# The convolution's banded matrices read from memory one by one, instead of being multiplied out on VectorE

## The chip, the cores and the metric

The kernel runs on one core of a Trainium2 chip. The metric is the device time of one execution in microseconds (us), lower is better. Three executions of the kernel before gave 2970.77, 2972.89 and 2979.89 us; the median is 2972.89 us. TensorE (PE in the profile) multiplies matrices, VectorE (DVE) and ScalarE (ACT) do the elementwise work, GpSimd (POOL) and SyncE (SP) mostly issue transfers. Each engine takes its own instructions in a fixed order.

## The reference, cut to what matters

Two layers over 1024 latent tokens and 256 context tokens, width 1024. The first layer's token mixer is a Conformer convolution module; the second is attention; each is followed by a SwiGLU feed-forward block. The change touches the depthwise convolution of the first layer alone:

```python
CONV_WIDTH = 31; CONV_PAD = 15
def conv_module(h, w_pw1, b_pw1, w_dw, b_dw, ln_g, ln_b, w_pw2, b_pw2):
    u = h @ w_pw1 + b_pw1                       # 1024 -> 2048
    a, gt = jnp.split(u, 2, axis=-1)
    u = a * jax.nn.sigmoid(gt)
    u = lax.conv_general_dilated(               # every channel has 31 taps of its own
        u, w_dw[:, None, :], window_strides=(1,), padding=[(15, 15)],
        dimension_numbers=("NWC", "WIO", "NWC"), feature_group_count=u.shape[-1]) + b_dw
    u = jax.nn.silu(layernorm(u, ln_g, ln_b))
    return u @ w_pw2 + b_pw2
```

All is float32. The kernel gets close to that precision by splitting every float32 operand of a product into a high part (a cast to TensorE's fp32r) and a low part (what is left), and adding three products: high by high, high by low, low by high.

## The kernel before, in words

**Convolution as products.** Tokens are stored by phase (token number modulo 8) and channels are taken in 64 groups of 16, so that 16 channels x 8 phases fill the 128 partitions. For one group the 31 taps become five 128x128 matrices (NM = 5 shifts), zero except where the channel of row and column agree. One such set of five, 128x640 numbers, is called a map here; there are 64 maps, numbered 0 to 63, and each is kept as a high and a low part.

**Where it stands.** `build` runs eight passes, k = 0 to 7. Pass k computes 128 features of the first projection (`pw1`: 3 pieces of the tokens C, L and R, with 256, 512 and 512 tokens) and in between, on the same TensorE, eight convolution steps of the group of features of the pass before. `conv` is a generator: step q asks `conv_maps` for the maps that come next, issues ten products with map q into one of three PSUM banks (`cv`), lets ScalarE move the sum out with the bias (L534, "the eviction") and VectorE add the second half (L536). The next step but two needs that bank again. In pass 7 steps 41 to 48 run; steps 49 to 63 follow with no projection beside them. After the last step come the LayerNorm of piece C and its product with `pw2` (L663).

**The look-ahead.** Maps are made two steps ahead, in a ring of three buffers in T6. In pass 7 the ring grows to six (`more_maps`, buffers in T1, which piece C of `pw1` has left) and then to nine (T2, which piece L has left). `conv` then asks for up to two maps a step, and `build` for one more at each of the last places of pass 7, until the ring is full; so maps 45 to 56 are asked for within the L and R pieces of pass 7, and the rest one a step.

**How a map is made before.** `conv_win` loads the taps of eight groups as a compact window (128x320, 160 KB, SP queue), casts it and subtracts (`split`: ScalarE's cast L159, VectorE's subtraction L162). Per map `conv_maps` spreads the high and the low window over the 16 channels by multiplying them with the 0/1 table `chan`: two VectorE multiplications of 128x640 (L504).

**What sets the order.** The program is written out line by line with generators, and a scheduler then places each engine's instructions by their priority (the place in the program) and readiness. It moves work within a few steps.

**Other names.** L470 copies the pass's features into the tile U (in KB), four DMAs from SP and four from ACT; `split_u` splits U (L159, L162 on HS). L460/L461 evict the projection. L142/L146 split projection weights. L270 (`mod_dve`) reduces a modulation weight on VectorE while the passes run. L563/L565 sum the convolution's result over channels. L608 (`load_cv`) reads the convolution's result back from DRAM: T<-vl for L and R, KB<-vc for C; KB<-vc goes into the place of U and of the raw window and so waits for their last reader. L592 subtracts the mean on VectorE.

Of the kernel before, what the change touches and what calls it, by code (L numbers as in the profile page):

```python
# [8 lines left out]
F32 = mybir.dt.float32  # L9
F32R = mybir.dt.float32r  # L10
I32 = mybir.dt.int32
AF = mybir.ActivationFunctionType
ALU = mybir.AluOpType
AX = mybir.AxisListType

P = 128
D = 1024
KT = D // P
# [10 lines left out]
EPS = 1e-6  # L29
MAGIC = float(0x5F3759DF)  # L30
CONST = (("cT", (KT, 2)), ("ident", (P,)), ("ones", (1,)), ("blk", (4,)), ("bmod", (2, 48)), ("ng", (2, 4, KT)),
         ("bpw1", (2 * KT,)), ("bcs", (KT * 8,)), ("selp", (8,)), ("chan", (16,)), ("lng", (KT,)), ("lnb", (KT,)), ("bpw2", (KT,)),
         ("qg", (2,)), ("kg", (2,)))
GROUPS = [list(range(i, min(i + GRP, FT))) for i in range(0, FT, GRP)]

# [1 line left out]
PH = 8  # L37
NM = 5
CG = 8
NC_, NL = CTX // PH, SEQ // PH  # L40
UW = 2 + NC_ + 2 + NL + 2
# [13 lines left out]
class Kern:  # L55
# [420 lines left out]
        u2 = self.u2[k % 2]  # L476
        self.split(u2[:, 0, g0:g1], u2[:, 1, g0:g1], self.U[:, g0:g1])

    def conv_win(self, k):

        if k < KT:
            self.split(self.cwin[0], self.cwin[1], self.craw)
        if k + 1 < KT:
            self.nc.sync.dma_start(self.craw, self.a["wwin"][k + 1])

    def more_maps(self, ring):

# [4 lines left out]
    def conv_maps(self):  # L492

        q = len(self.cwq)
        if q < KT * CG:
            if q % CG == 0:
                self.conv_win(q // CG)
            g = q % CG
            shape = [P, NM, 16, PH]
            self.cwq.append(self.cw[self.cwi % len(self.cw)])  # L500
            self.cwi += 1
            for t, w in zip(self.cwq[q], self.cwin):
                w = w[:, g * NM * PH:(g + 1) * NM * PH].bitcast(F32).rearrange("p (m s) -> p m s", s=PH)
                self.nc.vector.tensor_tensor(  # L504
                    t.rearrange("p (m c s) -> p m c s", c=16, s=PH),
                    w.unsqueeze(2).to_broadcast(shape), self.c["chan"].unsqueeze(1).unsqueeze(3).to_broadcast(shape),
                    op=ALU.mult)

    def conv(self):

# [548 lines left out]
    def build(self):  # L1059
        nc, a, c = self.nc, self.a, None  # L1060
        self.consts()
        c = self.c
        hs = {b: [] for b in PIECES}
# [61 lines left out]
        self.vsum = hr[:, TOK + nv + 2048:TOK + nv + 2048 + OW]  # L1125
        ut = self.T("HS", [P, 2, 2, CG, UW], F32R)
        self.u2 = [ut[:, i] for i in range(2)]
        kt = self.T("KB", [P, CG * UW + CG * NM * PH + 1024])
        self.U = kt[:, :CG * UW].rearrange("p (g n) -> p g n", g=CG)
        nw = CG * NM * PH  # L1130
        self.craw = kt[:, CG * UW:CG * UW + nw]
        mraw = kt[:, CG * UW + nw:]
        q = self.room()
        self.cwin = [q[:, o:o + nw].bitcast(F32R) for o in (0, 512)]
        cw = self.T("T6", [P, 6, NM * P], F32R)
        self.cw = [(cw[:, 2 * i], cw[:, 2 * i + 1]) for i in range(3)]
        self.cwq, self.cwi = [], 0
        for o, n in ((0, 2), (2 + NC_, 2), (UW - 2, 2)):
            nc.gpsimd.memset(self.U[:, :, o:o + n], 0.0)
        modg = self.mod_dve(range(16, 40), cr, (mraw, None), self.ps[:, 5:7].rearrange("p a b -> p (a b)"))  # L1140
        nc.vector.tensor_copy(self.craw[:, 0:1], hs["R"][0][1][:, KT - 1, 0:1].bitcast(F32))
        nc.sync.dma_start(self.craw, a["wwin"][0])
        self.conv_maps()
        cg = self.conv()
        for k in range(KT):
# [106 lines left out]
        hs = self.T("HS", [P, 4, 512])  # L1252
# [18 lines left out]
    def attention(self, final, qr):  # L1271
# [116 lines left out]
        for g in tails:  # L1388
# [1 line left out]
                pass  # L1390


NAMES = ("xT", "cst", "crow", "wmod", "wmodT", "pw1", "wwin", "pw2", "wq", "wk", "wv", "wo", "w1", "w3", "w2",
         "cos", "sin")


def layout(x, c, ctx, c_ctx, w_mod, b_mod, norm_g,
           conv_w_pw1, conv_b_pw1, conv_w_dw, conv_b_dw, conv_ln_g, conv_ln_b, conv_w_pw2, conv_b_pw2,
           attn_wq, attn_wk, attn_wv, attn_wo, attn_q_g, attn_k_g, ffn_w1, ffn_w3, ffn_w2):
    A = np.asarray  # L1400

    def feat(v):
        v = A(v)
        v = v.reshape(*v.shape[:-1], -1, P)
        return np.moveaxis(v, -1, 0)

    def wt(w):
        w = A(w)
        f = w.shape[1] // P
        return w.reshape(KT, P, f, P).transpose(2, 1, 0, 3).reshape(f, P, KT * P)  # L1410

    def phases(v, axis=0):
        v = np.moveaxis(A(v), axis, 0)
        v = v.reshape(-1, PH, *v.shape[1:]).swapaxes(0, 1).reshape(v.shape)
        return np.moveaxis(v, 0, axis)

    tok = np.concatenate([phases(A(ctx)[0]), phases(A(x)[0])], 0)
    o = {}
    o["xT"] = tok.T.reshape(KT, P, TOK).transpose(1, 0, 2)
    o["cT"] = np.stack([A(c)[0], A(c_ctx)], 1).reshape(KT, P, 2).transpose(1, 0, 2)  # L1420
    wm = A(w_mod)
    o["crow"] = np.concatenate([A(c)[0], A(c_ctx)])[None]
    o["wmod"] = wt(wm[0])
    o["wmodT"] = wm.transpose(0, 2, 1).reshape(2, 48, P, D)
    o["bmod"] = feat(b_mod)
    o["ng"] = feat(norm_g)
    o["pw1"] = wt(A(conv_w_pw1)[0])
    o["bpw1"] = feat(A(conv_b_pw1)[0])

    m, r, s = np.ogrid[:NM, :PH, :PH]  # L1430
    j = 8 * (m - 2) + r - s + PAD
    taps = np.concatenate([A(conv_w_dw)[0], np.zeros((1, D), np.float32)], 0)[np.where((j >= 0) & (j < CW), j, CW)]

    o["wwin"] = taps.reshape(NM, PH, PH, KT, CG, 16).transpose(3, 5, 1, 4, 0, 2).reshape(KT, P, CG * NM * PH)
    o["bcs"] = np.repeat(A(conv_b_dw)[0].reshape(D // 16, 16), PH, 1).T
    o["lng"] = feat(A(conv_ln_g)[0])
    o["lnb"] = feat(A(conv_ln_b)[0])
    o["pw2"] = wt(A(conv_w_pw2)[0])
    o["bpw2"] = feat(A(conv_b_pw2)[0])

    def heads(w):
        w = A(w).reshape(D, -1, 4, 32, 2)
        return wt(w.transpose(0, 1, 4, 3, 2).reshape(D, -1))
    o["wq"] = heads(A(attn_wq)[0])
    o["wk"] = heads(A(attn_wk)[0])
    o["wv"] = A(attn_wv)[0].reshape(2, 4, P, 256).transpose(0, 2, 1, 3).reshape(2, P, 1024)
    o["wo"] = wt(A(attn_wo)[0])
    o["qg"] = np.repeat(A(attn_q_g)[0].reshape(32, 2), 4, 0)
    o["kg"] = np.repeat(A(attn_k_g)[0].reshape(32, 2), 4, 0)
    o["w1"] = np.stack([wt(w) for w in A(ffn_w1)])  # L1450
    o["w3"] = np.stack([wt(w) for w in A(ffn_w3)])
    w2 = A(ffn_w2).reshape(2, FT, P, 4, 2, P)
    o["w2"] = np.concatenate(
        [w2[:, g[0]:g[-1] + 1].transpose(0, 3, 2, 4, 1, 5).reshape(2, 4, P, -1) for g in GROUPS], -1)

    o["ident"] = np.eye(P, dtype=np.float32)
    o["blk"] = np.kron(np.ones((32, 1)), np.eye(4)).astype(np.float32)
    o["ones"] = np.ones((P, 1), np.float32)
    o["chan"] = np.kron(np.eye(P // PH), np.ones((PH, 1))).astype(np.float32)
    o["selp"] = np.kron(np.ones((P // PH, 1)), np.eye(PH) / D).astype(np.float32)  # L1460
    fr = np.float32(10000.0) ** (-np.arange(16, dtype=np.float32) / np.float32(16))
    t = np.arange(SEQ)
    ang = np.concatenate([(t // 64).astype(np.float32)[:, None] * fr, (t % 64).astype(np.float32)[:, None] * fr], 1)
    o["cos"] = phases(np.repeat(np.cos(ang).T, 4, 0).astype(np.float32), 1)
    o["sin"] = phases(np.repeat(np.sin(ang).T, 4, 0).astype(np.float32), 1)
    o["cst"] = np.concatenate([o[k].reshape(P, -1) for k, _ in CONST], 1)
    return {k: np.ascontiguousarray(o[k]) for k in NAMES}

# [16 lines left out]
```

## Time and profile before

| what | value |
| --- | --- |
| median of 3 executions | 2972.89 us (2970.77 to 2979.89) |
| the profiled execution | 2976.11 us, span 2974.2 us |
| instructions | 39039 |
| PE busy | 2892.7 us (97%) |
| DVE busy | 1924.1 us (65%) |
| ACT busy | 1196.7 us (40%) |
| POOL busy | 240.0 us (8%) |
| the chain that ended last | PE 89%, DVE 7% |

The profile is of one execution. Times inside it count from the start of its span. A row of the timeline gives start, duration, engine, line, operation, output and input tiles, shape, and in brackets how long the engine was idle before and what ended it. The passes of the convolution module lie between about 85 and 343 us, the remaining convolution steps end at 374 us, and the first product of `pw2` starts at 385.90 us.

### The profile page before, as it was taken

To read this page: it belongs to the slowest core of one execution; us is meant where nothing else is said; L and a number is where in the kernel's file an instruction comes from. 1 tells how busy PE (TensorE), PEld (TensorE's weight loads), DVE (VectorE), ACT (ScalarE), POOL (GpSimd) and SP (SyncE) were. 2 spreads that over 40 slices of the span, in tenths; PEclk is the share of its full clock that TensorE was granted. 3 is DMA by queue.
4 is the path that set the end of the run, shared out by engine and by line. 5 is a ranking of instruction groups with operands and counts; after the bars stand their busy time and mean duration, and the time that the engine had idled before them with its cause. 6 is when DMAs were issued, how large, how long until landed. Compare 5 with 4: busy or idle time off the path is not lost.

```text
span 2974.2 us, 39039 instructions
## 1 busy us (share of the span) xinstructions
PE 2892.7 (97%) x14970; PEld 2410.8 (81%) x14970; DVE 1924.1 (65%) x3390; ACT 1196.7 (40%) x1966; POOL 240.0 (8%) x387
## 2 busy tenths in 40 slices
PE   8999989999999999999999999989999999999997
PEld 6888877888888888888888777767777778888886
DVE  6887887857565367333567899786666657543335
ACT  5222265532222135222344788645555543332222
POOL 0000001011111010000013111100100000000000
PEclk9999999999999999999989999989999999999998
DMA  6443434334345244333445211322213143442332
GB/s 245 135 121 97 122 129 173 111 114 141 126 163 174 64 132 152 93 98 98 136 145 166 65 48 45 106 79 78 84 54 85 63 136 103 148 144 93 94 98 64
DMA packets 132138, 336.35 MB, mean 113 GB/s; under 512 B 31472, under 2 KB 53008, under 8 KB 130800
## 3 DMA queue, kind: packets, MB, share of 16 engines
q1 hardware_dynamic: 78624, 222.59, 23.5%
q0 software_dynamic: 29408, 103.83, 10.8%
q10 hardware_dynamic: 23920, 7.44, 1.1%
q8 instruction: 117, 1.92, 0.3%
q14 instruction: 69, 0.57, 0.1%
HBM read 289.50 MB, written 38.93 MB: 110 GB/s over the span
## 4 chain that ended last, share of the span: by engine, by line
PE 89%; DVE 7%; issue 1%; ACT 1%; DMA 1%; ACTq 0%; SPq 0%; DVEq 0%; POOL 0%
PE ps L170 21%; PE ps L171 20%; PE ps L172 20%; PE ps L984 4%; PE ps L1002 4%; PE ps L1008 2%; PE ps L1009 2%; PE ps L452 2%; PE ps L454 2%; PE ps L453 2%; PE ps L530 1%; PE ps L663 1%; PE ps L181 1%; PE ps L182 1%; PE ps L183 1%
## 5 line engine op out<-in xcount | busy, mean ns | idle before, releaser
L172 PE MATMUL ps<-T,wl 128*128 128x512 f32 (+1 forms) x2032 | 766.3, 377 | 5.6 <-DVE wl L146 5.6
L170 PE MATMUL ps<-T,wh 128*128 128x512 f32 (+1 forms) x2032 | 769.4, 379 | 0.6 <-DVE sm L806 0.4
L171 PE MATMUL ps<-T,wh 128*128 128x512 f32 (+1 forms) x1984 | 747.1, 377 | 0.0
L142 ACT CAST wh<-wr 128x1024 fp32r<-128x1024 f32 x285 | 299.2, 1050 | 744.2 <-PE ps L171 551.3
L146 DVE TENSOR_TENSOR wl<-wr,wh 128x1024 fp32r<-128x1024 f32 x279 | 341.4, 1224 | 278.8 <-ACT wh L142 273.8
L172 PEld LDWEIGHTS ps<-T,wl 128*128 128x128 f32 x2032 | 384.9, 189 | 75.5 <-DVE wl L146 6.1
L170 PEld LDWEIGHTS ps<-T,wh 128*128 128x128 f32 x2032 | 385.3, 190 | 69.9 <-ACT T L1345 1.7
L171 PEld LDWEIGHTS ps<-T,wh 128*128 128x128 f32 x1984 | 375.9, 189 | 66.5 <-DVE T L162 1.0
L171 PE MATMUL ps<-HS,wh 128*128 128x512 f32 (+1 forms) x768 | 298.0, 388 | 0.0
L1006 DVE TENSOR_TENSOR T<-ps,T 128x512 fp32r<-128x512 f32 x320 | 217.0, 687 | 111.8 <-ACT T L1005 111.0
L170 PE MATMUL ps<-HS,wh 128*128 128x512 f32 (+1 forms) x720 | 277.9, 388 | 0.0
L172 PE MATMUL ps<-HS,wl 128*128 128x512 f32 (+1 forms) x720 | 277.8, 386 | 0.0
L1005 ACT CAST T<-ps 128x512 fp32r<-128x512 f32 x320 | 185.8, 585 | 195.0 <-PE ps L1002 181.2
L1002 PE MATMUL ps<-cst,T 128*128 128x128 f32 x1100 | 190.3, 275 | 4.9 <-DVE T L1006 4.8
L990 DVE TENSOR_SCALAR_CACHE_REDUCE T<-ps,rq 128x1280 f32<-128x1280 f32 x110 | 170.1, 1546 | 27.4 <-PE ps L984 21.7
L837 DVE TENSOR_TENSOR T<-ps,T 128x512 f32<-128x512 f32 (+1 forms) x168 | 110.6, 664 | 116.7 <-PE ps L172 116.1
L1002 PEld LDWEIGHTS ps<-cst,T 128*128 128x128 f32 x1100 | 133.4, 141 | 51.5 <-DVE T L1006 32.4
L812 DVE TENSOR_TENSOR sm<-sm,ps 128x256 f32<-128x256 f32 (+1 forms) x88 | 54.6, 620 | 182.3 <-PE ps L172 182.2
L171 PEld LDWEIGHTS ps<-HS,wh 128*128 128x128 f32 x768 | 144.8, 188 | 27.4 <-DVE HS L162 0.2
L992 ACT ACTIVATE T<-T,mn 128x1280 f32<-128x1280 f32 x110 | 150.3, 1366 | 40.9 <-DVE T L990 40.4
L172 PEld LDWEIGHTS ps<-HS,wl 128*128 128x128 f32 x720 | 135.4, 188 | 26.8
L170 PEld LDWEIGHTS ps<-HS,wh 128*128 128x128 f32 x720 | 135.0, 188 | 26.1 <-ACT HS L159 0.8
(277 smaller groups left out, 4686.2 us busy)
## 6 DMA issues: line engine op xcount, KB each, us to landing
wr<-in_w SPq DMA_DIRECT2D x220, 512.0 KB, 3.5
q<-in_w SPq DMA_DIRECT2D x44, 512.0 KB, 3.4
wr<-in_pw SPq DMA_DIRECT2D x35, 512.0 KB, 3.7
HR<-in_wmodT POOLq DMA_DIRECT2D x56, 256.0 KB, 3.9
q<-in_wmodT POOLq DMA_DIRECT2D x56, 256.0 KB, 3.8
q<-qsd POOLq DMA_DIRECT2D x32, 256.0 KB, 3.4
wr<-in_wo SPq DMA_DIRECT2D x16, 512.0 KB, 3.3
qsd<-T POOLq DMA_DIRECT2D x14, 512.0 KB, 3.8
```

Source lines behind the costliest of these rows:

```text
L142: nc.scalar.copy(hi, raw)
L146: nc.vector.tensor_tensor(lo, raw, hi.bitcast(F32), op=ALU.subtract)
L170: nc.tensor.matmul(out[:, :n], lhsT=wh, rhs=xh, start=k == 0, stop=False)
L171: nc.tensor.matmul(out[:, :n], lhsT=wh, rhs=xl, start=False, stop=False)
L172: nc.tensor.matmul(out[:, :n], lhsT=wl, rhs=xh, start=False, stop=k == nk - 1)
L837: nc.vector.tensor_tensor(yd, out[:, :c1 - c0], yd, op=ALU.add)
L984: nc.tensor.matmul(sc[:, k0:k0 + w], lhsT=q[:, h, :], rhs=kt[:, p * TOK + k0:p * TOK + k0 + w], start=p == 0, stop=p == 1)
L990: nc.vector.tensor_scalar(out=pt, in0=sc, scalar1=rq[:, h:h + 1], scalar2=None, op0=ALU.mult, op1=ALU.min, accum_out=mn)
L992: nc.scalar.activation(pt, pt, AF.Exp, bias=mn, scale=-1.0, accum_out=sums[:, 0, h:h + 1])
L1002: nc.tensor.transpose(tp[:, h * P:(h + 1) * P], Ps[h][:, j * P:(j + 1) * P], c["ident"])
L1005: nc.scalar.copy(ph, tp)
L1006: nc.vector.tensor_tensor(pl, tp, ph.bitcast(F32), op=ALU.subtract)
```

## The change

The host lays out all 64 maps in full (`in_wmap`, 64 x 128 x 640 numbers, 21 MB) in place of the windows (`in_wwin`, 1.3 MB). `map_load` reads one map (320 KB) into one of two raw buffers in KB, as a DMA of the POOL queue; it is issued for map q + 2 as soon as map q is split, since they share a raw buffer. `conv_maps` makes a map by one `split` of it: a cast on ScalarE and one subtraction on VectorE. The windows, their split, the 0/1 table and the 128 multiplications go. The raw buffer of `mod_dve` moves from KB to the tile q. Line numbers move by up to ten: the eviction becomes L526, its addition L528, the copies L470 and `split` L159/L162 stay, L544 becomes L536, L563 becomes L555, L592 becomes L584, L608 becomes L600.

```diff
-    def conv_win(self, k):
-
-        if k < KT:
-            self.split(self.cwin[0], self.cwin[1], self.craw)
-        if k + 1 < KT:
-            self.nc.sync.dma_start(self.craw, self.a["wwin"][k + 1])
+    def map_load(self):
+
+        q = self.cwl
+        if q < KT * CG:
+            self.nc.gpsimd.dma_start(self.craw[q % len(self.craw)], self.a["wmap"][q])
+            self.cwl += 1
...
         q = len(self.cwq)
         if q < KT * CG:
-            if q % CG == 0:
-                self.conv_win(q // CG)
-            g = q % CG
-            shape = [P, NM, 16, PH]
             self.cwq.append(self.cw[self.cwi % len(self.cw)])
             self.cwi += 1
-            for t, w in zip(self.cwq[q], self.cwin):
-                w = w[:, g * NM * PH:(g + 1) * NM * PH].bitcast(F32).rearrange("p (m s) -> p m s", s=PH)
-                self.nc.vector.tensor_tensor(
-                    t.rearrange("p (m c s) -> p m c s", c=16, s=PH),
-                    w.unsqueeze(2).to_broadcast(shape), self.c["chan"].unsqueeze(1).unsqueeze(3).to_broadcast(shape),
-                    op=ALU.mult)
+            self.split(*self.cwq[q], self.craw[q % len(self.craw)])
+            self.map_load()
...
-        kt = self.T("KB", [P, CG * UW + CG * NM * PH + 1024])
+        kt = self.T("KB", [P, CG * UW + 2 * NM * P])
         self.U = kt[:, :CG * UW].rearrange("p (g n) -> p g n", g=CG)
-        nw = CG * NM * PH
-        self.craw = kt[:, CG * UW:CG * UW + nw]
-        mraw = kt[:, CG * UW + nw:]
-        q = self.room()
-        self.cwin = [q[:, o:o + nw].bitcast(F32R) for o in (0, 512)]
+        self.craw = [kt[:, CG * UW + i * NM * P:CG * UW + (i + 1) * NM * P] for i in range(2)]
+        mraw = self.room()
...
-        nc.vector.tensor_copy(self.craw[:, 0:1], hs["R"][0][1][:, KT - 1, 0:1].bitcast(F32))
-        nc.sync.dma_start(self.craw, a["wwin"][0])
+        for r in self.craw:
+            nc.vector.tensor_copy(r[:, 0:1], hs["R"][0][1][:, KT - 1, 0:1].bitcast(F32))
+            self.map_load()
         self.conv_maps()
```

TensorE's instructions stand in the same order as before. Those of ScalarE and VectorE do not; the prediction speaks of the end of pass 7. ScalarE there, before, from the projection's eviction of piece L on: evictions of convolution steps (L534), the projection's last eviction (second L460), the copies to U and the split of U.

```order
L460 ACTIVATE sm<-ps,cst 128x512
L534 ACTIVATE HR<-ps,cst 128x162
L159 CAST q<-KB 128x320
L534 ACTIVATE HR<-ps,cst 128x162
L544 DMA vc_88<-HR 128x8x32
L544 DMA vl_96<-HR 128x8x128
L460 ACTIVATE sm<-ps,cst 128x512
L470 DMA KB<-HR 128x1x128 x4
L534 ACTIVATE HR<-ps,cst 128x162 x2
L159 CAST HS<-KB 128x664 x2
L534 ACTIVATE HR<-ps,cst 128x162 x6
```

ScalarE at the same place now, from the projection's eviction of piece L to the copies of piece R into U; T_621, T_2727 and T_2815 are the three parts of the ring (T6, T1, T2), and the casts into them are those of maps 49 to 56.

```order
L460 ACTIVATE sm<-ps,cst 128x512
L159 CAST T_2815<-KB 128x640 x2
L526 ACTIVATE HR<-ps,cst 128x162
L159 CAST T_2815<-KB 128x640
L159 CAST T_621<-KB 128x640 x2
L526 ACTIVATE HR<-ps,cst 128x162
L159 CAST T_2727<-KB 128x640
L536 DMA vc_88<-HR 128x8x32
L536 DMA vl_96<-HR 128x8x128
L159 CAST T_2727<-KB 128x640 x2
L460 ACTIVATE sm<-ps,cst 128x512
L470 DMA KB<-HR 128x1x128 x4
```

Eight casts, each of which waits for its load, now stand ahead of the projection's last eviction and of the copies into U.

VectorE from the split of U's second half to the last map, before (the T rows are the last maps):

```order
L162 TENSOR_TENSOR HS<-KB,HS 128x664
L536 TENSOR_TENSOR HR<-HR,ps 128x162
L504 TENSOR_TENSOR T_2785<-q,cst 128x640 x2
L504 TENSOR_TENSOR T_621<-q,cst 128x640
L536 TENSOR_TENSOR HR<-HR,ps 128x162
L504 TENSOR_TENSOR T_621<-q,cst 128x640 x2
L536 TENSOR_TENSOR HR<-HR,ps 128x162
L504 TENSOR_TENSOR T_621<-q,cst 128x640
L504 TENSOR_TENSOR T_2698<-q,cst 128x640
L536 TENSOR_TENSOR HR<-HR,ps 128x162
L504 TENSOR_TENSOR T_2698<-q,cst 128x640
L536 TENSOR_TENSOR HR<-HR,ps 128x162
```

The same stretch now, to the first subtraction of the mean (L584):

```order
L162 TENSOR_TENSOR T_2815<-KB,T_2815 128x640 x2
L528 TENSOR_TENSOR HR<-HR,ps 128x162 x2
L162 TENSOR_TENSOR T_621<-KB,T_621 128x640 x2
L528 TENSOR_TENSOR HR<-HR,ps 128x162 x2
L555 TENSOR_REDUCE sm<-HR 128x162
L557 TENSOR_TENSOR HR<-HR,sm 128x162
L574 TENSOR_SCALAR part<-HR 128x32
L565 TENSOR_TENSOR sm<-part,cst 128x256
L162 TENSOR_TENSOR T_2727<-KB,T_2727 128x640
L528 TENSOR_TENSOR HR<-HR,ps 128x162 x2
L584 TENSOR_TENSOR KB<-KB,ps 128x256
```

The last map's subtraction has moved behind the sums over channels (L555 to L565), and the additions behind the evictions come in pairs after two maps each.

More of the change, by code (lines that the diff above doesn't have):

```diff
@@ L31 @@
 CONST = (("cT", (KT, 2)), ("ident", (P,)), ("ones", (1,)), ("blk", (4,)), ("bmod", (2, 48)), ("ng", (2, 4, KT)),
-         ("bpw1", (2 * KT,)), ("bcs", (KT * 8,)), ("selp", (8,)), ("chan", (16,)), ("lng", (KT,)), ("lnb", (KT,)), ("bpw2", (KT,)),
+         ("bpw1", (2 * KT,)), ("bcs", (KT * 8,)), ("selp", (8,)), ("lng", (KT,)), ("lnb", (KT,)), ("bpw2", (KT,)),
          ("qg", (2,)), ("kg", (2,)))
@@ L1127, in build @@
         self.u2 = [ut[:, i] for i in range(2)]
-        kt = self.T("KB", [P, CG * UW + CG * NM * PH + 1024])
+        kt = self.T("KB", [P, CG * UW + 2 * NM * P])
         self.U = kt[:, :CG * UW].rearrange("p (g n) -> p g n", g=CG)
-        nw = CG * NM * PH
-        self.craw = kt[:, CG * UW:CG * UW + nw]
-        mraw = kt[:, CG * UW + nw:]
-        q = self.room()
-        self.cwin = [q[:, o:o + nw].bitcast(F32R) for o in (0, 512)]
+        self.craw = [kt[:, CG * UW + i * NM * P:CG * UW + (i + 1) * NM * P] for i in range(2)]
+        mraw = self.room()
         cw = self.T("T6", [P, 6, NM * P], F32R)
         self.cw = [(cw[:, 2 * i], cw[:, 2 * i + 1]) for i in range(3)]
-        self.cwq, self.cwi = [], 0
+        self.cwq, self.cwi, self.cwl = [], 0, 0
         for o, n in ((0, 2), (2 + NC_, 2), (UW - 2, 2)):
@@ L1390, in attention @@
                 pass
-NAMES = ("xT", "cst", "crow", "wmod", "wmodT", "pw1", "wwin", "pw2", "wq", "wk", "wv", "wo", "w1", "w3", "w2",
+NAMES = ("xT", "cst", "crow", "wmod", "wmodT", "pw1", "wmap", "pw2", "wq", "wk", "wv", "wo", "w1", "w3", "w2",
          "cos", "sin")
@@ L1432, in layout @@
     taps = np.concatenate([A(conv_w_dw)[0], np.zeros((1, D), np.float32)], 0)[np.where((j >= 0) & (j < CW), j, CW)]
-    o["wwin"] = taps.reshape(NM, PH, PH, KT, CG, 16).transpose(3, 5, 1, 4, 0, 2).reshape(KT, P, CG * NM * PH)
+    taps = taps.reshape(NM, PH, PH, KT * CG, 16).transpose(3, 4, 1, 0, 2)
+    wmap = np.zeros((KT * CG, 16, PH, NM, 16, PH), taps.dtype)
+    for ch in range(16):
+        wmap[:, ch, :, :, ch] = taps[:, ch]
+    o["wmap"] = wmap.reshape(KT * CG, P, NM * P)
     o["bcs"] = np.repeat(A(conv_b_dw)[0].reshape(D // 16, 16), PH, 1).T
@@ L1458, in layout @@
     o["ones"] = np.ones((P, 1), np.float32)
-    o["chan"] = np.kron(np.eye(P // PH), np.ones((PH, 1))).astype(np.float32)
     o["selp"] = np.kron(np.ones((P // PH, 1)), np.eye(PH) / D).astype(np.float32)
```

## Prediction

> **What bounds the kernel now.** I read the page's busy times, then the stretches of the convolution module, then what TensorE waited for there.
>
> ```profile
> PE 2892.7 (97%) x14970; PEld 2410.8 (81%) x14970; DVE 1924.1 (65%) x3390; ACT 1196.7 (40%) x1966; POOL 240.0 (8%) x387
> ...
> 200.00:225.00 25.00, 23.59 (x121) 20.15 (x120) 18.71 (x31) 5.93 (x11) 0.00 (x0) 1.00 0.24 69
> ...
> 300.00:325.00 25.00, 25.00 (x155) 22.74 (x154) 19.33 (x29) 4.58 (x9) 0.00 (x0) 1.00 0.34 81
> 325.00:350.00 25.00, 23.66 (x135) 20.87 (x133) 19.59 (x30) 4.45 (x9) 0.00 (x0) 1.00 0.31 84
> 350.00:375.00 25.00, 19.19 (x122) 17.50 (x120) 22.55 (x47) 8.21 (x22) 0.00 (x0) 0.93 0.67 200
> 375.00:400.00 25.00, 16.50 (x64) 13.77 (x65) 20.01 (x53) 11.50 (x23) 0.00 (x0) 0.73 0.26 86
> ```
>
> TensorE is busy for 97% of the span. In the passes it has no gap at all in most windows (25.00 of 25.00 us; 1.41 us idle in 200 to 225), although VectorE makes maps there. A map that comes earlier cannot shorten these windows. Only from 343 us on, where no projection fills TensorE, is there room: it idles 1.34, 5.81 and 8.50 us in the last three windows.
>
> ```profile
> PE ps L575 <- DVE sm L573: 5.9, 2, 3.5
> PE ps L379 <- DVE nr L339: 4.4, 2, 3.5
> PE ps L530 <- DVE HR L536: 2.9, 4, 1.3
> ```
>
> TensorE's waits between 60 and 420 us are for VectorE: the sums over channels (L573), the statistics (L339), the additions that give a PSUM bank back (L536). The end looks like this on VectorE and TensorE:
>
> ```profile
> 316.96 3.02 DVE L504 TENSOR_TENSOR T<-q,cst 128x640 fp32r<-128x640 f32 x4
> ...
> 359.19 0.82 DVE L504 TENSOR_TENSOR T<-q,cst 128x640 fp32r<-128x640 f32 x1
> ...
> 364.71 1.41 DVE L592 TENSOR_TENSOR KB<-KB,ps 128x256 f32<-128x256 f32 x4 [0.69 <-PE ps L575]
> ...
> 374.98 0.32 DVE L536 TENSOR_TENSOR HR<-HR,ps 128x162 f32<-128x162 f32 x1 [0.97 <-ACT HR L534]
> ...
> 371.74 0.31 PE L530 MATMUL ps<-HS,T 128*128 128x324 f32 x1
> ...
> 373.05 0.31 PE L530 MATMUL ps<-HS,T 128*128 128x324 f32 x1
> ...
> 385.90 2.93 PE L663 MATMUL ps<-T,wr 128*128 128x256 f32 x6 [1.11 <-ACT T L644]
> ```
>
> Maps 45 to 63 are made from about 317 us on, the last is done at 360.0, the first mean is subtracted at 364.7, the last step's addition ends at 375.3, `pw2` starts at 385.9. A step that waits for nothing takes 373.05 - 371.74 = 1.31 us. So what the change is worth is decided between about 320 and 386 us, and the measure is when the last map is ready.
>
> **The change part by part.**
>
> ```profile
> L504 DVE TENSOR_TENSOR T<-q,cst 128x640 fp32r<-128x640 f32 x128 | 102.2, 820 | 8.3 <-PE ps L531 6.7 <-PE ps L454 1.1
> L162 DVE TENSOR_TENSOR q<-KB,q 128x320 fp32r<-128x320 f32 x8 | 3.9, 492 | 3.5 <-ACT q L159 3.4
> L159 ACT CAST q<-KB 128x320 fp32r<-128x320 f32 x8 | 3.7, 458 | 23.4 <-DVE T L504 20.2 <-DMA KB<-in_wwin 3.2
> L162 DVE TENSOR_TENSOR HS<-KB,HS 128x664 fp32r<-128x664 f32 x2 | 1.7, 846 | 0.0
> L159 ACT CAST HS<-KB 128x664 fp32r<-128x664 f32 x2 | 1.5, 748 | 1.1 <-DMA KB<-HR 1.1
> ...
> L391 DVE TENSOR_TENSOR acc<-acc,sb 128x256 f32<-128x256 f32 x8 | 3.4, 423 | 1.0 <-ACT sb L390 1.0
> L536 DVE TENSOR_TENSOR HR<-HR,ps 128x162 f32<-128x162 f32 x64 | 20.4, 319 | 13.9 <-ACT HR L534 13.9
> L563 DVE TENSOR_REDUCE sm<-HR 128x162 f32<-128x648 f32 x1 | 1.3, 1329 | 0.0
> ```
>
> VectorE loses 128 multiplications of 820 ns (105.0 us) and 8 window subtractions of 492 ns (3.9 us). It gains 64 subtractions of 128x640; between 492 ns at 320 and 846 ns at 664 columns that is 0.82 us each (52.5 us). ScalarE loses 8 casts of 458 ns and gains 64, between 458 and 748 ns: 0.73 us each (46.6 us); it is busy about 6 of 25 us in the passes. SP loses eight window loads, and `mod_dve`'s raw buffer and the two one-column copies ahead of the first loads change nothing that ends a wait. POOL, idle in all these windows, gains 64 issues. None of these busy times lies on the path while TensorE is full: in 85 to 343 us I cost them at nothing, and their cover is the projection's products; what it costs if that cover fails is the second rival below.
>
> ```profile
> 279.01 1.30 ACT L159 CAST HS<-KB 128x1328 fp32r<-128x1328 f32 x1 [4.22 <-DMA KB<-HR]
> ...
> 280.35 1.54 DVE L162 TENSOR_TENSOR HS<-KB,HS 128x1328 fp32r<-128x1328 f32 x1 [4.46 <-ACT HS L159]
> ```
>
> What is new is the load. Its round trip on one raw buffer is: issue to landing (call it L), cast 0.73, subtraction 0.82, and three hand-overs, from the subtraction to POOL, from the landing to the cast, from the cast to the subtraction. The last is 280.35 - 279.01 - 1.30 = 0.04 us in the split of U; for the two with a queue I allow 0.1 each, an estimate from that row. So a trip is L + 1.8 us, and there are two raw buffers. L is not in the trace; the nearest rows:
>
> ```profile
> L288 POOL DMA_DIRECT2D HR<-in_wmodT x56: 537/537/542, 607.6 to 934.0; - x56
> ...
> DMA to landing us min/median/max: 2.8/3.9/5.9
> ```
> ```profile
> L484 SPq DMA_DIRECT2D KB<-in_wwin x7: 328/333/337, 86.0 to 322.9; - x7
> ...
> DMA to landing us min/median/max: 2.1/2.2/2.9
> ```
> ```profile
> L608 SPq DMA_DIRECT2D T<-vl x16: 332/430/1193, 342.9 to 379.7; - x16
> ...
> DMA to landing us min/median/max: 2.0/4.5/5.6
> ```
> ```profile
> DMA  5826003010000838899878421343000533254444
> ```
>
> The first is the same queue with 256 KB: 2.8 to 5.9, median 3.9 us, taken while weights stream. The second is 160 KB from SP: 2.1 at least. The third is 256 KB from SP just where the passes end: median 4.5, at most 5.6. The last row is the busy share from 300 to 420 us in slices of 3 us: nearly nothing from 309 to 339, 80 to 90% from 342 to 366. So L lies between 2.1 and 5.9 us; I take 3.3 while the DMA engines are idle (between the first row's fastest and its median, for a load a quarter larger) and 4.2 beside the traffic after 342.
>
> The Trainium skill ("DMA: Bandwidth & Descriptors", Anatomy of one DMA - SWDGE (gpsimd) path) fits 2.0 us plus bytes over 436 GB/s for a DMA of this queue, 2.75 us for 320 KB. By that, the sum below would give +1 us instead of +7.5. The trace does not quite follow it: its fastest 256 KB load takes 2.8 us where the fit says 2.6, and the median 3.9.
>
> *In the passes* a raw buffer is used every second step.
>
> ```profile
> 301.24 0.37 ACTq L544 DMA_DIRECT2D vc<-HR  x1
> ...
> 338.52 0.38 ACTq L544 DMA_DIRECT2D vc<-HR  x1
> ```
> ```profile
> 266.68 0.31 PE L530 MATMUL ps<-HS,T 128*128 128x324 f32 x1
> ...
> 273.59 0.31 PE L530 MATMUL ps<-HS,T 128*128 128x324 f32 x1
> ```
>
> Eight steps take 338.52 - 301.24 = 37.3 us, two 9.3 on average and 273.59 - 266.68 = 6.9 at the closest, against a trip of 3.9 + 1.8 = 5.7. It fits, with two steps of look-ahead as reserve. Behind a waiting cast on ScalarE stand the evictions, but a bank is needed again only three steps later. I take 0, with up to -1.4 (the gap in 200 to 225 goes) in the range.
>
> *From the middle of pass 7* the look-ahead grows and the program asks for nineteen maps in a row, 45 to 63: 43 us of VectorE's time before, with other work in between, now nineteen loads. Maps 49 to 51 go into T2, free once TensorE has left piece L:
>
> ```profile
> 329.48 0.69 ACT L460 ACTIVATE sm<-ps,cst 128x512 f32<-128x512 f32 x1 [2.34 <-PE ps L454]
> ...
> 343.13 0.69 ACT L460 ACTIVATE sm<-ps,cst 128x512 f32<-128x512 f32 x1 [5.11 <-PE ps L454]
> ```
>
> ScalarE waited for TensorE until 329.48 there. One eviction (0.69), two casts and their subtractions behind it, and map 49 is done at 331.8, map 50 at 332.5. From then on each odd map is one trip behind the last: 51 to 63, seven trips. Two before the traffic, two after it, 4 x (3.3 + 1.8) = 20.4, three in it, 3 x (4.2 + 1.8) = 18.0: the last map is done at 331.8 + 38.4 = 370.2, against 360.0. VectorE, whose 14 multiplications after 344 become 7 subtractions, does not limit this: it would save 7 x 0.8 = 5.6 us there and waits instead.
>
> Queued behind the waiting casts on ScalarE are the projection's last eviction (343.13 before, about 347.5 now), the copies into U and the evictions; so steps 51 to 58 run in bursts, each when a bank comes free. They are ahead of map 63 all the same: step 58 is done by then, where before step 57 had just begun, so this costs nothing of its own. KB<-vc must now wait for the last map, as KB holds the raw buffers; its issue and landing (0.4 + at least 2.0, with hand-overs and some traffic 3.2 us) replace the 364.7 - 360.0 = 4.7 us of sums, now done ahead: -1.5. From the first subtraction of the mean to the last addition it took 375.3 - 364.7 = 10.6 us, paced by seven steps of TensorE. Now VectorE's own work sets it: 7 means at 0.35 (1.41 for four, above), 6 squares at 0.35 and 7 additions at 0.25 (each row less the same overlap of 0.07), sums of 1.3 and about 0.7, in all 8.3, plus 1.1 for step 63, whose bank waits for an addition near the end of that row: 9.4, so -1.2. What follows is as before. Sum: +10.2 - 1.5 - 1.2 = +7.5 us.
>
> The profiled execution took 2976.11 us, so 2983.6 by the sum; it is 3.2 above the median, 2972.89, on whose scale the forecast is 2980.4 us.
>
> **The rivals.**
>
> *Slower, loads in the traffic.* From 342 to 366 the read-back of L and R, the store of vl and the maps share the DMA engines. If four trips meet L = 5.6 (the third row's longest) and three 3.3, the last map is done at 331.8 + 29.6 + 15.3 = 376.7: +16.7 - 2.7 = +14.0, 2986.9 us. More than 0.3% (8.9 us, about what a measurement of this kernel can tell from no change) follows once the mean of the seven L is over 3.9, the first row's median. For it: the row of slices and that median; against: the loads before 342 find idle engines.
>
> *Slower, in every pass.* If L exceeds 6.9 - 1.8 = 5.1 us, two close steps don't cover a trip, the cast holds ScalarE, and with it evictions and the next map. At 5.9 it is 0.8 us short, some twice a pass, over six passes 9.6 us on top of the tail's 7.5: 2990. Against it: slices at 0 to 3 tenths between 309 and 339, and the reserve of two steps.
>
> *No net loss.* At L = 2.6 the last map comes at 331.8 + 7 x 4.4 = 362.6 and the later gains cancel it: 2973. At 2.1 it is -3.6 and, with the gap in 200 to 225 closed, 2968. For it: the loads of 160 KB land in 2.1 to 2.9.
>
> *Faster.* If loads never delay a map, the steps run at 1.31 us from 343: 16 x 1.31 ends them at 363.9 instead of 374.4, and with the gap -11.9: 2961. It needs a trip below 2 x 1.31, so L under 0.8, which no row comes near.
>
> **How the numbers follow.** The forecast's case, +1 to +8.9, has 0.42; no net loss 0.15; the traffic 0.25; every pass 0.12; faster 0.06. Faster by over 0.3%: 0.06; within 0.3%: 0.42 + 0.15 = 0.57; slower: 0.37. The range runs from 2968 (L at its lower bound) to 2993 (every load at the 5.9 of the first row: 331.8 + 7 x 7.7 = 385.7, +23, of which I keep 20, since the traffic ends at 366). It leaves out 0.06 below and about 0.07 above.
>
> **What would show it.** In the profile after: TensorE without gaps up to 325 (step one); 64 casts of 128x640 near 0.73 us and as many subtractions near 0.82 (the prices); in_wmap landing in 3.3 to 4.2 us (the new term); casts that wait for in_wmap between 330 and 370 and not before; the last 128x640 subtraction near 370 and `pw2` near 393. I am wrong if ScalarE waits for in_wmap in the passes, if gaps of TensorE appear before 325, or if the last map is done before 362.

## The result, and the profile after

The changed kernel takes 2998.63 us, the median of six executions (2995.30 to 3003.95), beside 2972.98 us of the kernel before (six, 2970.77 to 2979.89): a ratio of 1.0079, 95% interval 1.0066 to 1.0091, 25.65 us slower. The forecast was 2980.4 us, 7.5 us slower, with a range up to 2993; the time lies beyond it. The profiled execution is the slowest of the six (3003.95 us, span 3002.2); read its places, not its total.

The page after, its busy times and the row of the new load (KB each, median us from issue to landing):

```profile
PE 2903.2 (97%) x14970; PEld 2415.9 (80%) x14970; DVE 1876.3 (62%) x3319; ACT 1234.9 (41%) x2022; POOL 273.8 (9%) x451
...
KB<-in_wmap POOLq DMA_DIRECT2D x64, 320.0 KB, 3.5
```

VectorE has 47.8 us less to do, ScalarE 38.2 more. The same stretches as before the change (length, busy time of PE, PEld, DVE, ACT and POOL, clock, DMA share, GB/s):

```profile
200.00:225.00 25.00, 24.30 (x141) 21.48 (x140) 14.79 (x26) 7.94 (x15) 3.23 (x6) 1.00 0.60 180
300.00:325.00 25.00, 25.00 (x160) 22.89 (x159) 11.92 (x16) 8.37 (x14) 2.69 (x5) 1.00 0.54 137
325.00:350.00 25.00, 25.00 (x132) 21.64 (x131) 10.36 (x16) 8.70 (x15) 4.85 (x9) 1.00 0.40 112
350.00:375.00 25.00, 13.28 (x64) 12.11 (x62) 9.66 (x15) 7.93 (x15) 2.69 (x5) 0.70 0.79 250
375.00:400.00 25.00, 18.35 (x92) 17.24 (x92) 17.39 (x41) 8.14 (x21) 1.08 (x2) 0.75 0.46 128
400.00:425.00 25.00, 18.02 (x73) 14.90 (x73) 18.62 (x50) 12.40 (x25) 0.00 (x0) 0.73 0.29 85
```

TensorE is full until 350. In the three stretches behind that it idles 11.7, 6.7 and 7.0 us, at clocks of 0.70 to 0.75; before it was 5.8 and 8.5 from 350 to 400, at 0.93 and 0.73. VectorE, which was busy for 22.55 us of 350 to 375, is busy for 9.66: it has become idle, not fast. The waits after, from 325 to 410 us (us in total, times, longest):

```profile
ACT T L159 <- DMA KB<-in_wmap: 30.6, 12, 5.3
DVE T L162 <- ACT T L159: 25.3, 12, 5.1
...
PE ps L522 <- DVE HR L528: 13.1, 4, 6.9
```

The cast waits for the load, the subtraction for the cast, and TensorE for a bank. In single rows, from several engines (SPq stands for transfers that SyncE issues):

```profile
343.07 0.54 POOL L483 DMA_DIRECT2D KB<-in_wmap  x1 [3.81 <-DVE T L162]
348.16 0.54 POOL L483 DMA_DIRECT2D KB<-in_wmap  x1 [3.69 <-DVE HR L528]
348.89 3.22 SPq L600 DMA_DIRECT2D T<-vl  x4
349.37 0.54 POOL L483 DMA_DIRECT2D KB<-in_wmap  x1 [0.67 <-DVE T L162]
354.43 0.54 POOL L483 DMA_DIRECT2D KB<-in_wmap  x1 [4.51 <-DVE T L162]
357.38 0.72 ACT L159 CAST T<-KB 128x640 fp32r<-128x640 f32 x1 [4.11 <-DMA KB<-in_wmap]
358.01 0.68 ACT L460 ACTIVATE sm<-ps,cst 128x512 f32<-128x512 f32 x1
362.70 0.40 ACT L526 ACTIVATE HR<-ps,cst 128x162 f32<-128x162 f32 x1 [3.71 <-PE ps L525]
362.99 1.34 ACT L159 CAST T<-KB 128x640 fp32r<-128x640 f32 x2
364.76 3.96 SPq L600 DMA_DIRECT2D T<-vl  x6
364.86 0.54 POOL L483 DMA_DIRECT2D KB<-in_wmap  x1 [5.06 <-DVE T L162]
371.61 0.72 ACT L159 CAST T<-KB 128x640 fp32r<-128x640 f32 x1 [5.25 <-DMA KB<-in_wmap]
373.49 0.54 POOL L483 DMA_DIRECT2D KB<-in_wmap  x1 [7.36 <-DVE T L162]
378.68 0.54 POOL L483 DMA_DIRECT2D KB<-in_wmap  x1 [2.54 <-DVE T L162]
384.60 0.83 DVE L162 TENSOR_TENSOR T<-KB,T 128x640 fp32r<-128x640 f32 x1
387.71 0.42 DVE L584 TENSOR_TENSOR KB<-KB,ps 128x256 f32<-128x256 f32 x1
```

An undisturbed trip goes from issue to issue on one raw buffer, 343.07 to 348.16: 5.1 us. Beside the read-backs (T<-vl) the load issued at 349.37 is cast only at 357.38, 8.0 us later; the one of 364.86 at 371.61. The last map is done at 385.43, the first mean is subtracted at 387.71, and `pw2` starts at 409.08 instead of 385.90, +23.2.

Where these 23.2 us lie: 1.7 stand ahead of any instruction that the change touches; 4.3 come in the passes, so the projection's last matmul starts 6.0 later; 17.2 come between it and `pw2`. That last stretch, from the start of the last L452 to the start of the first product of `pw2`, is called the tail below: 43.7 us before, 60.9 after.

### The profile page after: what moved, and what is told of

It is laid out like the page before. It is cut to its first block, busy times and chain, and to the rows that moved or that the text cites. A ratio compares the mean times of both kernels' runs of the same rounds, so it can differ in the third digit from the quotient of the medians.

```text
span 3002.2 us, 39246 instructions
## 1 busy us (share of the span) xinstructions
PE 2903.2 (97%) x14970; PEld 2415.9 (80%) x14970; DVE 1876.3 (62%) x3319; ACT 1234.9 (41%) x2022; POOL 273.8 (9%) x451
```

## The experiments

| kernel | last L452 | first `pw2` | tail | time against before, 95% interval |
| --- | --- | --- | --- | --- |
| before | 342.2 | 385.9 | 43.7 | 1 |
| after | 348.2 | 409.1 | 60.9 | 1.0079 (1.0066 to 1.0091) |
| no_reload | 341.8 | 382.7 | 40.9 | 0.9990 (0.9979 to 1.0001) |
| back_behind | 343.9 | 402.1 | 58.2 | 1.0098 (1.0083 to 1.0112) |
| six_raws | 342.7 | 385.5 | 42.8 | 1.0014 (1.0003 to 1.0026) |
| first_cast_later | 347.2 | 406.7 | 59.5 | 1.0089 (1.0075 to 1.0103) |
| quiet | 345.2 | 404.0 | 58.8 | 1.0073 (1.0060 to 1.0086) |
| two_raws | 345.7 | 395.9 | 50.2 | 1.0035 (1.0022 to 1.0048) |
| no_tie | 345.1 | 404.8 | 59.7 | 1.0054 (1.0042 to 1.0067) |
| late_ring | 343.1 | 404.9 | 61.8 | 1.0069 (1.0056 to 1.0082) |
| half_loads | 344.9 | 397.9 | 53.0 | 1.0038 (1.0024 to 1.0053) |
| swap_queues | 348.6 | 406.7 | 58.1 | 1.0054 (1.0034 to 1.0073) |
| six_no_tie | 342.9 | 385.2 | 42.3 | 1.0005 (0.9994 to 1.0016) |

The columns in us are from one profiled execution each; the three kernels whose instructions stand in the same order at the end and whose loads are the same (after, first_cast_later, no_tie) give tails of 59.5 to 60.9, so a us or two in this column says little. The times are ratios to executions of the kernel before that were taken anew beside each run. 0.1% is 3 us.

**no_reload: are the loads the cause?**

```diff
-        if q < KT * CG:
+        if q < 2:
             self.nc.gpsimd.dma_start(self.craw[q % len(self.craw)], self.a["wmap"][q])
```

> Only maps 0 and 1 are loaded; maps 2 to 63 are cast and subtracted from the data left in the two raw buffers, so the convolution uses wrong matrices: the part left out is 62 loads of 320 KB. Everything else (casts, subtractions, ring, order) is as in the changed kernel. Theory A (the loss is the two raw buffers' round trip with the loads in the traffic of the last pass): with no load in the chain the last subtraction follows the last eviction of the projection within about 20 us instead of 27, the 23 us of the tail and the 4 us at 90 us are gone, and the time is that of the kernel before or less, 2962 to 2976 us. Theory B (the loss is in the place and the engine of the work: casts on ScalarE in front of evictions, subtractions on VectorE): the loads don't matter and the time stays at 2990 us or more.

The time is 0.9990 of before and the tail 40.9 us. With the casts and subtractions kept, the whole loss is gone: it is the loads' (theory A). Their order, though, was not kept: without loads ScalarE has five casts instead of eight between the projection's evictions of L and R, and behind the latter casts and evictions alternate, where after has them in pairs. The order is not what made the difference: six_raws has the eight casts and a tail of 42.8, and swap_queues alternates too and has 58.1. The same run shows what the removed multiplications bring when no load is in the way: the tail is 2.8 us shorter than before, and the time hardly differs.

**back_behind: the read-backs out of the way, first try.**

```diff
-                        self.load_cv(b, j)
+                        self.load_cv(b, j, self.nc.sync if b == "C" else self.nc.gpsimd)
```

> The fourteen read-backs of vl (L and R, channel blocks 0 to 6, 256 KB each) are issued by POOL behind the last map load instead of by SP beside the map loads. Theory A1 (a trip grows because the read-backs share the DMA engines with the map load): landings in the tail fall from up to 8.1 us to 3.3 to 4.4, the last map is done near 375 instead of 385 us, and the time falls by 8 to 11 us, to 2988 to 2991. Theory A2 (the tail's landings are long for another reason, the stores of vl and the reloads of the window or POOL's own issue): unchanged, 2996 to 3001.

No gain in the time, but the edit did not do what was meant: the read-backs did not wait behind the last map load, they went between the loads on POOL.

```profile
352.60 0.54 POOL L483 DMA_DIRECT2D KB<-in_wmap  x1 [2.06 <-DVE T L162]
353.18 2.65 POOL L600 DMA_DIRECT2D T<-vl  x5
358.01 0.54 POOL L483 DMA_DIRECT2D KB<-in_wmap  x1 [2.18 <-DVE T L162]
```

So it tells A1 from A2 in neither direction. Its tail is 2.7 us shorter than that of after, and yet its time isn't; why is open.

**six_raws: many loads in flight.**

```diff
+                        t3 = self.T("T3", [P, 6, NM * P])
+                        self.more_raws([t3[:, j] for j in range(6)])
...
+    def more_raws(self, new):
+        n = len(self.craw)
+        self.craw = new + [self.craw[(self.cri + i) % n] for i in range(n)]
+        self.cri = 0
+        for _ in new:
+            self.map_load()
```

> Six more raw buffers in T3, which is free once the last pass's L piece is done, with their six loads issued there at once. Theory A (the round trip through two buffers is what the tail waits for): the loads of maps 53 to 58 overlap one another, the wait of the convolution for the last maps is gone, the last addition falls back from 398.5 to 375 to 382 us, and the time to 2974 to 2982 us. Theory A' (what bounds the tail is the DMA engines' bytes, not the trip): eight loads and the read-backs share the same engines and the tail gains less than 8 us, 2990 us or more. Theory B (casts and subtractions in the way of evictions): 2996 us or more.

Theory A: 1.0014, tail 42.8 us. This run also shows what was scarce. Its loads from 325 to 345 us, and those of after from 346 to 376 (KB each, median us to landing):

```profile
T<-in_wmap POOLq DMA_DIRECT2D x11, 320.0 KB, 5.9
KB<-in_wmap POOLq DMA_DIRECT2D x3, 320.0 KB, 7.0
```
```profile
KB<-in_wmap POOLq DMA_DIRECT2D x8, 320.0 KB, 4.3
```

A load takes longer with eight buffers (5.9 to 7.0 us) than with two (4.3), and the loss is gone all the same, since the loads overlap. They also ran at another time. The windows 325 to 340 and 340 to 360, before, after and six_raws:

```profile
325.00:340.00 15.00, 15.00 (x80) 12.99 (x79) 13.32 (x21) 2.34 (x5) 0.00 (x0) 1.00 0.04 6
340.00:360.00 20.00, 16.83 (x109) 14.91 (x108) 16.27 (x27) 4.92 (x11) 0.00 (x0) 1.00 0.83 247
```
```profile
325.00:340.00 15.00, 15.00 (x80) 13.05 (x79) 5.59 (x10) 5.49 (x10) 2.70 (x5) 1.00 0.39 101
340.00:360.00 20.00, 13.08 (x75) 11.44 (x74) 9.22 (x12) 5.54 (x9) 3.23 (x6) 0.92 0.59 194
```
```profile
325.00:340.00 15.00, 15.00 (x80) 12.97 (x80) 7.48 (x12) 7.38 (x14) 6.52 (x13) 1.00 0.72 243
340.00:360.00 20.00, 17.36 (x106) 16.05 (x105) 13.77 (x24) 9.42 (x19) 0.94 (x2) 0.91 0.93 276
```

From 325 to 340 the DMA engines lay idle before (share 0.04); two buffers used them at 0.39, eight at 0.72. From 340 to 360 they were less busy after (0.59) than before (0.83), but this mean hides two opposite stretches:

```profile
349.00:357.00 8.00, 3.99 (x31) 3.76 (x29) 3.72 (x4) 0.73 (x1) 1.08 (x2) 0.98 1.00 320
357.00:361.00 4.00, 1.09 (x5) 1.09 (x5) 1.72 (x3) 1.60 (x3) 0.54 (x1) 0.50 0.22 50
```

While the load of 349.37 was under way, the DMA engines were full (1.00, 320 GB/s). Right behind it they fell to 0.22, with six loads still to be issued and at most one in flight, for want of a free buffer. The loss has both sides: traffic that makes a load long, and idle DMA engines that two buffers can't use.

**first_cast_later: the gap in the first passes.**

```diff
+                if k == 1 and i == 6:
+                    self.conv_maps()
```

> The first map's cast and subtraction are put in the program in the middle of pass 1 (behind its sixth step) instead of ahead of pass 0; the loads stay where they are. Theory (ScalarE, held by the first cast, which waits for a load of 8.1 us, lets the evictions of pass 0 come late): TensorE's gap of 2.1 us at 90.7 us is gone and all that follows is earlier by 2 to 4 us: 2994 to 2997 us. Rival (the pass made up for it, or the two casts wait again where they stand now): 2998 to 3000 us.

This run says nothing on the cause: the scheduler placed the cast in ScalarE's order where it had been (it ran at 85.30 us), and only the source moved. (The 8.1 us of the expectation are the longest landing of the whole run, issued at 365.59; the first two loads of after landed in 3.7 and 5.0 us.) It serves as a second execution of nearly the same order: tail 59.5, passes 5.0 us longer.

**quiet: the read-backs held until the last map.**

```diff
                     self.cvs[b] = self.T(t, [P, KT, PIECES[b][1] - PIECES[b][0]])
+                    if b != "C":
+                        nc.vector.tensor_copy(self.cvs[b][:, :KT - 1, 0:1], self.cwq[KT * CG - 1][1][:, 0:KT - 1].bitcast(F32).unsqueeze(2))
```

> The read-backs of vl for L and R are held until the last map is done: VectorE writes one column of their target from the last map's low part, and the read-backs, which write the same place, wait for it. The orders of ScalarE, POOL and TensorE are those of the changed kernel. The stretch from the projection's last matmul to the first of pw2 was 43.7 us before the change and 60.9 after it. Theory T (the traffic of the read-backs makes the trips long): landings in that stretch at 3.2 to 4.4 us, the last map done by 374 us instead of 385, the stretch 50 to 53 us, and the time lower by 6 to 10 us if the late read-backs cost nothing behind it: 2989 to 2993. Theory R (the trip through two buffers is long even without them, since casts wait in ScalarE's order in front of evictions): the stretch stays at 57 us or more, 2996 us or more.

Half of each theory. The issues on one raw buffer, the last map and, later, the wait that took its place:

```profile
351.35 0.54 POOL L483 DMA_DIRECT2D KB<-in_wmap  x1 [4.48 <-DVE T L162]
359.31 0.54 POOL L483 DMA_DIRECT2D KB<-in_wmap  x1 [4.92 <-DVE T L162]
365.25 0.54 POOL L483 DMA_DIRECT2D KB<-in_wmap  x1 [4.67 <-DVE T L162]
370.50 0.54 POOL L483 DMA_DIRECT2D KB<-in_wmap  x1 [3.93 <-DVE T L162]
375.00 0.82 DVE L162 TENSOR_TENSOR T<-KB,T 128x640 fp32r<-128x640 f32 x1
379.19 5.76 SPq L602 DMA_DIRECT2D T<-vl  x11
395.58 0.42 DVE L586 TENSOR_TENSOR KB<-KB,ps 128x256 f32<-128x256 f32 x1 [5.31 <-DMA KB<-HR]
```

The last map is done at 375.8 us, 9.6 earlier than after, 3.0 of them from the passes. Seven trips took 40.9 us against 47.5, so the read-backs cost them 6.6. But the tail, 58.8 us, and the time are about those of after: the fourteen read-backs now run from 379 on, ahead of the last step's copies KB<-HR, for which VectorE then waits 5.3 us. The traffic was moved, not saved.

**two_raws: how many buffers.** As six_raws, with `range(2)`.

> As six_raws, but with two more raw buffers instead of six, four in all. Trips of 5 to 8 us then carry four maps instead of two. If the trip is all: 13 maps behind the end of the ring's free part need four trips instead of seven, the stretch from the projection's last matmul to pw2 falls from 60.9 to 46 to 50 us, and the time to 2980 to 2988. If the gain of six_raws came only from loads that were issued before the last pass ended: less than half of the 18 us, 2990 us or more. If two more are already enough: 2976 to 2980.

Tail 50.2, time 1.0035 (2987.93 us): the upper end of what was expected if the trip is all. With 2, 4 and 8 buffers the tail is 60.9, 50.2 and 42.8 us, and 40.9 with no loads.

**no_tie: the first loads earlier.**

```diff
         for r in self.craw:
-            nc.vector.tensor_copy(r[:, 0:1], hs["R"][0][1][:, KT - 1, 0:1].bitcast(F32))
             self.map_load()
```

> The two copies that tie the first map loads to the end of the norm of R are left out, so that the first loads are issued as soon as their space is free, some 30 us earlier. If the gap of TensorE at 90 us (1.1 to 3.8 us, with the clock at 0.66 for 5 us behind the longer ones) comes from the first cast, which waits on ScalarE for a load of 4 to 8 us, the gap goes and the passes are 1 to 5 us shorter: 2994 to 2998 us. If the gap comes from the window's own traffic at 85 to 90 us: 2998 to 3001 us.

TensorE's gap at the first maps, after and here:

```profile
90.67 0.80 PE L452 MATMUL ps<-T,wh 128*128 128x512 f32 x1 [2.13 <-ACT sm L460]
```
```profile
87.75 0.50 PE L452 MATMUL ps<-T,wh 128*128 128x512 f32 x1 [0.84 <-ACT sm L460]
```

The gap shrinks, and the time falls to 1.0054; the interval only just touches that of after. The passes are 2.3 us longer than before here, where after had 4.3. But the nine profiles whose passes begin as those of after (it, and all kernels but no_reload, no_tie and six_no_tie) show 0.3 to 5.2 for them, so the size of the tie's gain isn't settled.

**late_ring: fewer casts ahead of the projection's last eviction.** Both `more_maps` and the extra `conv_maps` of pass 7 are moved behind the passes:

```diff
-                if k == KT - 1 and i == 4:
-                    cw = self.T("T1", [P, 6, NM * P], F32R)
-                    self.more_maps([(cw[:, 2 * j], cw[:, 2 * j + 1]) for j in range(3)])
...
+        for t in ("T1", "T2"):
+            cw = self.T(t, [P, 6, NM * P], F32R)
+            self.more_maps([(cw[:, 2 * j], cw[:, 2 * j + 1]) for j in range(3)])
```

> The ring of map pairs grows from 3 to 9 only behind the last pass of the projection, so that the maps ahead are asked for later and fewer casts stand on ScalarE in front of the projection's last eviction. Theory R (the casts that wait for loads hold up that eviction, and it the split of U and the last convolution steps): the eviction follows the last matmul within 2 us instead of 9.5, and the time falls by 5 us or more, to 2986 to 2993. Theory trip (thirteen maps through two buffers set the end, wherever they stand): the maps start later, the end is later by 0 to 10 us, 2998 to 3009 us.

```profile
345.68 0.68 ACT L460 ACTIVATE sm<-ps,cst 128x512 f32<-128x512 f32 x1
```

The eviction comes at 345.68 instead of 358.01, as planned, and it doesn't help: tail 61.8, time 1.0069 (2997.53 us). The last map is done 38.8 us behind the start of the last L452, where after it was 37.2, and the tail follows it. So theory R falls as the account of the loss: with an early eviction the maps still set the end. As the edit also asks for the maps later, what the early eviction alone is worth isn't shown.

**half_loads: bytes or the trip itself.**

```diff
+            n = NM * P if q < 51 else NM * P // 2
-            self.nc.gpsimd.dma_start(self.craw[q % len(self.craw)], self.a["wmap"][q])
+            self.nc.gpsimd.dma_start(self.craw[q % len(self.craw)][:, :n], self.a["wmap"][q][:, :n])
```

> Maps 51 to 63 are loaded only for their first 320 of 640 columns (160 KB instead of 320); the other half is cast from old data, so half of those matrices is left out. If the length of a trip lies in the bytes and the shared DMA engines: a trip of 5.1 to 8 us falls to 3.5 to 5, the stretch from the projection's last matmul to pw2 from 60.9 to 48 to 53 us, the time to 2984 to 2991. If it lies in what every load costs whatever its size (issue, landing, hand-overs): the stretch stays above 56 us, 2994 us or more.

Tail 53.0, time 1.0038, at the upper end of what the bytes were to give. Half the bytes take off 7.9 of the 17.2 us. From 346 to 385 us the landing is 2.4 us at the fastest, against 3.2 for the full load, and still 7.6 at the longest; two trips still took 7.0 and 7.7 us, where 3.5 to 5 were expected. So bytes are a part of it, and not the whole.

**swap_queues: who issues.**

```diff
-            self.nc.gpsimd.dma_start(self.craw[q % len(self.craw)], self.a["wmap"][q])
+            (self.nc.sync if q >= 53 else self.nc.gpsimd).dma_start(self.craw[q % len(self.craw)], self.a["wmap"][q])
...
-                        self.load_cv(b, j)
+                        self.load_cv(b, j, self.nc.gpsimd)
```

> The loads of maps 53 to 63 are issued by SP and the read-backs of vc and vl (channel blocks 0 to 6) by POOL, the other way round than in the changed kernel. If POOL's queue is what makes the loads long: landings fall below 3 us without traffic and below 5 with it, the stretch from the projection's last matmul to pw2 is 50 to 55 us instead of 60.9, 2986 to 2993 us. If it is the two buffers and the shared DMA engines, whoever issues: 57 to 64 us, 2995 to 3002 us.

Landings of the map loads from 346 to 385 us, after and here:

```profile
DMA to landing us min/median/max: 3.2/4.3/8.1
```
```profile
DMA to landing us min/median/max: 2.9/3.3/7.0
```

SP's loads land a little sooner, and the longest is still 7.0; the tail is 58.1, within the 57 to 64 us expected if the issuer doesn't matter. That is what the Trainium skill says ("DMA: Bandwidth & Descriptors", Issuing engines are not separate DMA queues): transfers of all issuers interleave on the same 16 engines.

**six_no_tie: both edits that helped.** six_raws and no_tie together.

> Six more raw buffers in T3 for the last pass, and the first two loads without their tie: the two edits that helped, together. If their gains add up (18 to 20 us in the tail, 4 to 7 us in the passes): 2970 to 2976 us beside 2976 of the kernel before, a ratio of 0.998 to 1.000, level with the kernel before or a little faster. If the tie's gain was one of the tail's: 2977 to 2981 us. Faster than 0.998 isn't expected, since with no loads at all the ratio was 0.999.

1.0005, level with the kernel before. The interval reaches over that of six_raws, so the gains of the two aren't shown to add up. The changed kernel can be mended, and no version that beats the kernel before came of it; no_reload shows that little is to be had.

## Why the prediction was wrong

**Right: the place and the mechanism.** The change decides between 320 and 386 us, and the measure is when the last map is ready. From 100 to 348 us TensorE was busy for 245.8 of 248 us, as before (245.3). The prices hold:

```profile
L162 DVE TENSOR_TENSOR T<-KB,T 128x640 fp32r<-128x640 f32 x64 | 52.4, 822 | 47.7 <-ACT T L159 47.4
L159 ACT CAST T<-KB 128x640 fp32r<-128x640 f32 x64 | 46.0, 721 | 54.8 <-DMA KB<-in_wmap 54.6
```

So does the start of the seven trips: maps 49 and 50 are done at 337.7 and 338.4, which less the 6.0 of the passes is 331.7 and 332.4 (forecast 331.8 and 332.5). An undisturbed trip takes 5.1 us, as forecast (3.2 for the landing, 1.9 for the rest).

**Wrong: the three trips in the traffic.** The step that failed is "three in it, 3 x (4.2 + 1.8) = 18.0". From issue to issue on that buffer (337.98, 343.07, 348.16, 354.43, 364.86, 373.49, 378.68, done 385.43) the trips took 5.1, 5.1, 6.3, 10.4, 8.6, 5.2 and 6.8 us: 47.5 in all against 38.4. The three in the traffic took 25.3 us instead of 18.0, the last one 1.7 more than an undisturbed trip because its subtraction (384.60) stood behind the sums over channels. L was too small: I took it from landing rows of the kernel before, at most 5.9 us, and so did every rival; but those were the landings beside the old traffic, and the map loads came on top of it. On this buffer the three loads landed in 4.3, 4.4 and 6.7 us, 2.8 more than 3 x 4.2; on the other one L reached 7.6 and 8.1. The larger error, 4.5 us, is in the 1.8 for the rest of the trip, which allowed for no wait in ScalarE's queue (next paragraph). quiet prices the traffic: 6.6 of the 9.1 us go when the read-backs do. The first rival named this traffic. Its threshold, a mean L over 3.9, was passed by the seven loads' 4.0; but it had the whole price in L, so that its 14.0 us come near the tail's 17.2 is partly luck.

**Wrong: "so this costs nothing of its own".** The load of 354.43 was cast only at 362.99, behind an eviction that had waited for TensorE (362.70 above). It had landed after 4.4 us, at 358.8, and lay in its buffer for some 4 us. The two buffers are tied through ScalarE: the load of 349.37, on the other buffer, took 7.6 us; ScalarE stood before its cast until 357.38 with evictions behind it, so TensorE waited for a bank until 359.91, and its step was evicted only at 362.70. A cast that is ready stands in ScalarE's order too, and the raw buffer is held meanwhile: without read-backs, in quiet, the same trip is still the longest, 8.0 us.

**Wrong: from the mean to the last addition, -1.2.** It took 398.48 - 387.71 = 10.8 us, as before (10.6). I had put VectorE there as the limit, with step 58 done by the last map; but step 57 was evicted only at 386.88, so TensorE still had its steps to do, at a clock of 0.50 from 385 to 390. The reload of KB<-vc gave 2.4 instead of 1.5: 387.71 - 385.43 = 2.3 us from the last map to the first mean, where before it was 4.7. So the tail is 7.5 as forecast, plus 9.1 for the trips, 1.4 for the mean, less 0.9, and 0.1 of rounding: 17.2.

**Wrong: the passes at 0.** They took 4.3 us more in this execution (0.3 to 5.2 in nine profiles, see no_tie). The trip does fit two steps: casts did wait for in_wmap in the passes, my sign of being wrong (19.5 us in six waits from 100 to 325), but TensorE's busy time above shows that these waits cost almost nothing. What I hadn't looked at was the first load, in a stretch where the DMA share is 0.95 (85 to 90 us): the first two casts, which wait for their loads, stand on ScalarE ahead of an eviction (89.94) that TensorE needs, and it waits 2.13 us. That the other gaps of the passes add to it isn't shown.

**Open.** In the profiled execution 4.8 more us come behind `pw2`: 3.6 up to 1143 us, part of it in gaps of 0.9 and 0.7 us at 548, the rest later, where executions of the other kernels move by several us either way. Whether they belong to the change isn't settled.

## What to carry to other kernels

A transfer that takes the place of arithmetic is not costed by its engine's busy time, nor by its landing in an old trace: count the buffers in flight, since the rate is buffers over the whole trip (issue, landing, each reader's place in its queue), and add the new bytes to the traffic before reading off L. Ask for the data in the stretch where the DMA engines lie idle; eight buffers made slower loads harmless. And a VectorE that is busy for 80% beside a full TensorE is no bound: from 100 to 348 us it was busy for 152.2 us instead of 198.9, and TensorE for 245.8 instead of 245.3.

## What was unexpected of the hardware

TensorE's clock halves behind a long wait. The gap of 6.92 us, the granted clock around it and one product of a step behind it:

```profile
359.91 0.64 PE L522 MATMUL ps<-HS,T 128*128 128x324 f32 x1 [6.92 <-DVE HR L528]
```
```profile
355.00:360.00 5.00, 0.09 (x1) 0.09 (x1) 1.72 (x3) 1.60 (x3) 0.54 (x1) 0.67 0.47 185
360.00:365.00 5.00, 4.19 (x16) 3.84 (x17) 1.59 (x3) 2.25 (x4) 0.14 (x1) 0.50 0.78 187
```
```profile
361.45 0.55 PE L522 MATMUL ps<-HS,T 128*128 128x324 f32 x1
```

The product takes 0.55 us where it took 0.31 before (371.74 there). The Trainium skill ("TensorE: Matmul & The Clock Gate", Part 1) has the clock fall to half after an idle window of about 3.4 us; this gap is longer, and the row agrees. Where the limit lies isn't settled here: behind the gap of 2.13 us at 90.67 the clock is 0.66 from 90 to 95 us, and behind gaps of 2.25 and 2.30 us in quiet and swap_queues it is 1.00. A late map thus costs twice, the wait and the slow steps behind it.
